# Decoder layer on one Trainium2 core: the opening eight blocks all split, its rows scaled token by token, and raw weights in eight half-size buffers

## The chip, the cores and the metric

The kernel runs on one core of one Trainium2 chip. The metric is device time in microseconds (us) of one execution; the numbers below are medians over executions, and one execution was profiled. TensorE (PE, with its weight loads PEld), VectorE (DVE), ScalarE (ACT), GpSimd (POOL) and SyncE (SP) each work through a queue of their own in program order. All weights come in by DMAs that SP issues.

## The reference

```python
mod = silu(c) @ w_ada + b_ada                      # nine vectors of 1024
sh1, sc1, g1, sh2, sc2, g2, sh3, sc3, g3 = split(mod, 9)
u = rmsnorm(x, norm_ff1) * (1 + sc1) + sh1         # x: 256 tokens x 1024
h = x + 0.5 * g1 * ((silu(u @ w_gate) * (u @ w_up)) @ w_down)     # 2816 hidden columns
u = rmsnorm(h, norm_mix) * (1 + sc2) + sh2
h = h + g2 * token_mixing(u)                       # linear attention and block attention
u = rmsnorm(h, norm_ff2) * (1 + sc3) + sh3
h = h + 0.5 * g3 * swiglu(u)                       # a second feed-forward of the same size
return rmsnorm(h, norm_final)
```

All is float32. The kernel reaches that precision by splitting each operand into a rounded high part and the low part that is left, and summing three products: high x high, high x low, low x high.

## The kernel before

Columns of the model lie on partitions in eight blocks of 128 (k = 0 to 7), tokens along the free axis. A weight tile goes through three steps: a DMA brings it into a raw buffer (`raw`), ACT rounds it (`hi`), DVE subtracts (`lo`). There are four raw buffers of 1 MB and six pairs of `hi` and `lo` of half that width. `split` does the rounding and the subtraction, `mm3` the three matmuls; `Stream` does it for all later weights, two halves to a raw buffer.

This study is about the opening, which here is called the lead. Its input is x, and the first 16 column tiles (8 gate, 8 up) of the first feed-forward. The vectors sc1 and sh1 are needed block by block, so for each k the lead loads 1 MB of `w_ada` (in two loads, `a` pieces), forms two dot products on DVE with `silu(c)` spread over all partitions (`cact`; `ada_dot`), and adds the bias and multiplies the norm weight in (`lead_mods`). It loads 1 MB of gate and up weights in two pieces (`l`), of which 14 column tiles are split and two are used as plain float32 (`lead_native`: TensorE shows two instructions for each). Eight PSUM banks collect all 16 tiles over k.

At the start x is transposed on TensorE into `h`, the square sums of both token tiles give 1/rms (`rstd`: DVE, then POOL), which two more transposes spread over partitions. Then for each block: `lead_normed` (DVE) multiplies by 1/rms, `lead_u` (ACT) applies scale and shift, `lead_uh` (ACT) rounds, `lead_ul` (DVE) subtracts, `lead_mm` runs the matmuls. The string `LEADING` sets the program order of these steps, `LOADS` that of the loads. The lead ends when the matmuls of block 7 are done; the next feed-forward tiles, then down projections, mixing and the second feed-forward follow without a break on TensorE. `mix_constants` and the `w_ada` loads of later vectors (`AdaQueue`) run beside them.

Of the kernel before, what the change touches and what calls it, by code (L numbers as in the profile page):

```python
# [23 lines left out]
NATIVE = 2  # L24
WARM = 5
LOADS = """a00 a01 l00 l01 a10 a11 l10 l11 a20 a21 l20 l21 a30 a31 l30 l31 a40 a41 l40 l41 a50 a51 l50 l51 a60
         a61 l60 l61 a70 a71 l70 l71"""
LEADING = """h00 m0 n0 c0 r00 v0 u0 b t n1 h01 r01 h10 d10 d11 m1 u1 c1 r10 v1 n2 h11 r11 x00 x01 p0 h20 d20 d21 m2
         u2 c2 r20 v2 n3 h21 r21 p1 x10 x11 h30 d30 d31 m3 u3 c3 r30 v3 n4 h31 r31 p2 x20 x21 h40
         d40 d41 m4 u4 c4 r40 v4 n5 h41 r41 p3 x30 x31 h50 d50 d51 m5 u5 c5 r50 v5 n6 h51 r51 p4 x40  # L30
         x41 h60 d60 d61 m6 u6 c6 r60 v6 n7 h61 r61 p5 x50 x51 h70 d70 d71 m7 u7 c7 r70 v7 h71 r71
         p6 x60 x61 A A p7 x70 x71"""
# [8 lines left out]
RAW = 4  # L41
# [36 lines left out]
def hybrid_layer(ctx: ExitStack, tc: tile.TileContext, x, cols, ident_d, tri_d, mask_d, onehot_d,  # L78
                 relT, wlr, ada, lead, gu1, dn1, win, gv, mv, gbr, wout, gu2, dn2, out):
# [80 lines left out]
    def raw_tile():  # L160
        return wp.tile([P, 4 * GV], F32, tag="raw", name=name("raw"), bufs=RAW)

    def load(src, width=2048, parts=1):
        t = raw_tile()
        for i in range(parts):
            sl = slice(i * width // parts, (i + 1) * width // parts)
            nc.sync.dma_start(t[:, sl], src[:, sl] if parts > 1 else src)
        return t

    def split(raw, lo, width=1024, later=False, gap=False):  # L170
# [3 lines left out]
        src, to_hi, to_lo = raw[:, lo:lo + width], hi[:, :width], low[:, :width]  # L174
# [41 lines left out]
    class Stream:  # L216


        def __init__(self):
            self.todo, self.ready, self.raw = [], [], {}  # L220

        def add(self, key, src, which, width=D, parts=1):
            self.todo.append((key, src, which, width, parts))
# [5 lines left out]
        def prepare(self):  # L229
            key, src, which, width, parts = self.todo.pop(0)  # L230
            if key not in self.raw:
                self.raw[key] = load(src, 2 * width, parts)
            self.ready.append(split(self.raw[key], which * width, width, gap=key[0] not in ("gv", "mv")))
# [41 lines left out]
    for t in range(2):  # L275
        nc.sync.dma_start(xt[:, t * D:(t + 1) * D], x[blk(t)])  # L276
    ident = cst.tile([P, P], F32, name="ident")
# [17 lines left out]
    for s in (1, 4, 7):  # L295
        vec.tensor_scalar(bada[:, s, :], bada[:, s, :], 1.0, None, op0=ALU.add)

    cact = cst.tile([P, D], F32, name="cact")
    pc = [bank(), bank()]
    for i in range(KD):  # L300
        ten.transpose(pc[i // 4][:, blk(i % 4)], csil[:, i:i + 1].to_broadcast([P, P]), ident)


    sq, ssq = [mid([P, D]), mid([P, D])], row((P, 8), tag="tiny", bufs=4)
# [35 lines left out]
    class AdaQueue:  # L340
# [5 lines left out]
        def step(self, n=1):  # L346
            for _ in range(n):
# [3 lines left out]
                raw = load(ada[4 * s + q])  # L351
                ada_dot(raw, 0, s, 2 * q)
                ada_dot(raw, D, s, 2 * q + 1)
# [221 lines left out]
    def ada_load(k, i):  # L575
        if i == 0:
            ada_raw[k] = raw_tile()
        sl = slice(0, D) if i else slice(D, 2 * D)
        nc.sync.dma_start(ada_raw[k][:, sl], ada[k, :, sl])  # L579

    def lead_load(k, i):
        if i == 0:
            lead_raw[k] = raw_tile()
        mid_c = (NATIVE + half) * P
        sl = slice(mid_c, N2 * P) if i else slice(0, mid_c)
        nc.sync.dma_start(lead_raw[k][:, sl], lead[k, :, sl])
# [14 lines left out]
    def lead_mods(k):  # L601
        vec.scalar_tensor_tensor(mods[:, 1, k:k + 1], gemv[:, 1, k:k + 1], bada[:, 1, k:k + 1],
                                 colt[:, C_N1 + k:C_N1 + k + 1], op0=ALU.add, op1=ALU.mult)
        vec.tensor_tensor(out=mods[:, 0, k:k + 1], in0=gemv[:, 0, k:k + 1], in1=bada[:, 0, k:k + 1], op=ALU.add)


    def lead_normed(k):
        if k:
            vec.tensor_tensor(out=xn[:, k, :S], in0=h[:, k, :S], in1=lead_rb[0][:, :S], op=ALU.mult)
        else:  # L610
            vec.scalar_tensor_tensor(xn[:, 0, :S], h[:, 0, :S], mods[:, 1, 0:1], rb[:, :S], op0=ALU.mult, op1=ALU.mult)

    def lead_u(k):
        us[k] = row(tag="u", bufs=3)
        act.activation(us[k], xn[:, k, :S], AF.Identity, scale=mods[:, 1, k:k + 1] if k else 1.0, bias=mods[:, 0, k:k + 1])

    def lead_uh(k):
        if k:
            act.activation(uh[:, k, :S], us[k], AF.Copy)
        else:  # L620
            act.activation(uh[:, 0, :S], xn[:, 0, :S], AF.Identity, bias=mods[:, 0, 0:1])

    def lead_ul(k):
        if k:
            vec.tensor_tensor(out=ul[:, k, :S], in0=us[k], in1=uh[:, k, :S], op=ALU.subtract)
        else:
            vec.scalar_tensor_tensor(ul[:, 0, :S], xn[:, 0, :S], mods[:, 0, 0:1], uh[:, 0, :S], op0=ALU.add,
                                     op1=ALU.subtract)
# [3 lines left out]
    def lead_high(k, i):  # L632
        lead_load_until(f"l{k}{i}")
        ws[k, i], rests[k, i] = split(lead_raw[k], (NATIVE + i * half) * P, half * P, True)
# [4 lines left out]
    def lead_native(k):  # L639
        for i in range(NATIVE):  # L640
            b = lead_banks[i // 2]
            mm(b[:, i % 2 * S:(i % 2 + 1) * S], b, lead_raw[k][:, blk(i)], us[k], stop=(k == KD - 1))

    def lead_mm(k, w):
        def to(at):
            i = NATIVE + w * half + at
            return lead_banks[i // 2][:, i % 2 * S:(i % 2 + 1) * S], lead_banks[i // 2]

        if k or w:
            for at in range(half):  # L650
                mm3(*to(at), ws[k, w], blk(at), (uh[:, k, :S], ul[:, k, :S]), stop=(k == KD - 1))
        else:

            for part, rows in ((0, uh), (1, uh), (0, ul)):
                for at in range(half):
                    mm(*to(at), ws[0, 0][part][:, blk(at)], rows[:, 0, :S])

    def lead_rbs():
        act.activation(rbs, rb[:, :S], AF.Copy)
        lead_rb[0] = rbs  # L660

    lead_load_until(to_load[2 * RAW - 1])
    work1 = []
    for f in range(LEAD, NF):
        stream.unit(("gu1", f), gu1[f - LEAD], parts=2 if f == LEAD else 1)
        work1.append(("f", f))
        n = sum(1 for x, _ in work1 if x == "d")
        if n < NF // 2 - 1 and 2 * n + 1 <= f - 2:
            stream.unit(("dn1", n), dn1[n], parts=1 if n else 2)
# [619 lines left out]
```

## Time and profile before

| | |
|---|---|
| median of 3 runs | 572.75 us (571.64 to 572.92) |
| the profiled execution, own time | 572.64 us |
| its span, first to last instruction | 570.9 us |
| TensorE busy | 557.3 us (98%) |
| VectorE busy | 442.8 us (78%) |
| ScalarE busy | 300.8 us (53%) |
| moved by DMA | 140.95 MB, 247 GB/s over the span |

The span leaves out 1.7 us of the execution's own time. Matmul ends are modelled in the profile, so distances between starts say more than TensorE's busy share.

### The profile page before, as it was taken

Reading aid. Unit: us, or ns where it says so; the run is one execution under the profiler, and the core shown is the slowest. Engines: PE = TensorE matmul, PEld = TensorE weight load, DVE = VectorE, ACT = ScalarE, POOL = GpSimd, SP = SyncE. Lnnn points to the kernel's source line nnn. Section 1 sums busy time; section 2 is a strip of 40 time slices with the busy share of each in tenths; the row PEclk is TensorE's granted clock in tenths of the full one; section 3 lists DMA queues with packets and bytes.
Section 4 is the critical chain, followed back from the end, with each engine's and each line's share of the span. In section 5 each row is a group of like instructions: output and inputs, shape, how many; then the busy total and the mean of one; then the engine's idle time right before and its main releaser. Section 6 shows DMA issues by size and latency. Waiting matters only on the chain.

```text
span 570.9 us, 11312 instructions
## 1 busy us (share of the span) xinstructions
PE 557.3 (98%) x4711; PEld 550.1 (96%) x4711; DVE 442.8 (78%) x701; ACT 300.8 (53%) x480; POOL 10.8 (2%) x14
## 2 busy tenths in 40 slices
PE   4999999999999999999999999999999999999996
PEld 3999999999999999998999999999999999999995
DVE  4999887879887896899998979789874656665534
ACT  5455664352536577843764544576644454345424
POOL 0000000000000010000001000001000000000000
PEclk9999999999999999999999999999999999999999
DMA  8999689898989726544489776842796566775102
GB/s 311 357 409 394 255 314 383 302 359 325 325 313 338 242 75 249 193 140 157 130 307 365 287 265 251 309 152 84 284 342 205 195 212 205 254 266 180 67 1 75
DMA packets 23237, 140.95 MB, mean 247 GB/s; under 512 B 2781, under 2 KB 3346, under 8 KB 8850
## 3 DMA queue, kind: packets, MB, share of 16 engines
q1 hardware_dynamic: 22722, 139.37, 67.6%
q8 instruction: 37, 0.61, 0.4%
q0 software_dynamic: 176, 0.53, 0.3%
q10 hardware_dynamic: 288, 0.33, 0.2%
q14 instruction: 14, 0.11, 0.1%
HBM read 139.16 MB, written 1.05 MB: 246 GB/s over the span
## 4 chain that ended last, share of the span: by engine, by line
PE 61%; issue 32%; DVE 4%; DMA 2%; SPq 0%; POOL 0%; ACT 0%; POOLq 0%; DVEq 0%
PE b L103 61%; DMA raw<-in_lead 2%; DVE b L103 1%; DVE lo L103 1%; DVE s L103 1%; DVE raw L103 0%; POOL tiny L363 0%; ACT hi L103 0%; SPq L579 0%; SPq L276 0%; POOLq L1284 0%; DVEq L1284 0%; ACT ub L103 0%; SPq L273 0%; DVE tiny L103 0%
## 5 line engine op out<-in xcount | busy, mean ns | idle before, releaser
L103 PE MATMUL b<-ub,hi 128*128 128x256 f32 (+1 forms) x1888 | 329.3, 279 | 3.2 <-ACT ub L103 3.2
L103 PEld LDWEIGHTS b<-ub,hi 128*128 128x128 f32 x1888 | 286.6, 189 | 5.1 <-ACT ub L103 3.4
L103 DVE TENSOR_TENSOR lo<-raw,hi 128x1024 fp32r<-128x1024 f32 (+2 forms) x188 | 223.2, 1211 | 66.6 <-ACT hi L103 65.1
L103 PE MATMUL b<-ub,lo 128*128 128x256 f32 (+1 forms) x944 | 261.1, 278 | 0.0
L103 ACT ACTIVATE hi<-raw 128x1024 fp32r<-128x1024 f32 (+2 forms) x188 | 191.5, 1044 | 83.4 <-issue 34.4
L103 PEld LDWEIGHTS b<-ub,lo 128*128 128x128 f32 x944 | 177.6, 189 | 0.0
L103 PE MATMUL b<-s,hi 128*128 128x256 f32 x960 | 165.4, 277 | 0.0
L103 PEld LDWEIGHTS b<-s,hi 128*128 128x128 f32 x960 | 144.8, 188 | 0.0
L103 PE MATMUL b<-s,lo 128*128 128x256 f32 x480 | 132.7, 277 | 0.0
L103 PEld LDWEIGHTS b<-s,lo 128*128 128x128 f32 x480 | 90.1, 188 | 0.0
L103 DVE SCALAR_TENSOR_TENSOR raw<-raw,cact 128x1024 f32<-128x1024 f32 x72 | 85.0, 1219 | 2.5 <-DMA raw<-in_ada 2.2
L103 ACT ACTIVATE s<-m 128x256 fp32r<-128x256 f32 x52 | 21.4, 417 | 76.7 <-DVE m L103 76.7
L103 ACT ACTIVATE sg<-b 128x256 f32<-128x256 f32 x46 | 17.0, 379 | 44.9 <-PE b L103 42.9
L103 DVE TENSOR_TENSOR s<-m,s 128x256 fp32r<-128x256 f32 x52 | 21.8, 424 | 20.6 <-ACT s L103 20.5
L103 DVE TENSOR_TENSOR m<-sg,b 128x256 f32<-128x256 f32 x43 | 17.8, 416 | 12.5 <-ACT sg L103 12.2
L103 ACT ACTIVATE s<-b 128x256 f32<-128x256 f32 (+5 forms) x33 | 13.9, 469 | 22.0 <-PE b L103 19.6
L103 PE MATMUL b<-hi,ub 128*128 128x264 f32 (+1 forms) x96 | 21.8, 321 | 0.0
L103 PEld LDWEIGHTS b<-hi,ub 128*128 128x128 f32 x96 | 15.8, 188 | 1.2
L103 PE MATMUL b<-lo,ub 128*128 128x264 f32 (+1 forms) x48 | 15.4, 321 | 0.0
L103 DVE SCALAR_TENSOR_TENSOR b<-b,mods,b 128x256 f32<-128x256 f32 x25 | 11.0, 477 | 4.7 <-PE b L103 4.6
L363 POOL TENSOR_TENSOR tiny<-tiny,mhalf 128x2 f32<-128x2 f32 (+1 forms) x5 | 7.1, 1418 | 365.5 <-DVE tiny L103 365.5
L103 ACT ACTIVATE sq<-b 128x256 f32<-128x256 f32 x24 | 9.2, 407 | 5.6 <-DVE b L103 5.2
(122 smaller groups left out, 276.4 us busy)
## 6 DMA issues: line engine op xcount, KB each, us to landing
raw<-in_gu SPq DMA_DIRECT2D x35, 1024.0 KB, 5.3
raw<-in_ada SPq DMA_DIRECT2D x28, 1024.0 KB, 6.1
raw<-in_dn SPq DMA_DIRECT2D x21, 1024.0 KB, 4.9
raw<-in_win SPq DMA_DIRECT2D x12, 1024.0 KB, 6.4
raw<-in_ada SPq DMA_DIRECT2D x16, 512.0 KB, 7.4
raw<-in_gbr SPq DMA_DIRECT2D x8, 1024.0 KB, 7.2
raw<-in_lead SPq DMA_DIRECT2D x8, 576.0 KB, 6.3
raw<-in_wout SPq DMA_DIRECT2D x4, 1024.0 KB, 5.9
```

Of the source, the lines that this page charges most:

```text
L103: x = getattr(self.engine, op)(*args, **kw)
L363: nc.gpsimd.tensor_tensor(out=rs[:, :n], in0=ms[:, :n], in1=mhalf[:, :n], op=ALU.pow)
```

## The change

Nothing is native any more: the 16 column tiles of each lead block are all split, as two halves of eight (`lead_mm`), with the 32-element gap in the middle of the `hi` and `lo` tiles that the other weights already had. The loads of the lead's `w_ada` rows carry two more columns (input `adal`, rows of 1026 elements) that hold bias and one; `cact` ends in two ones, and the norm weight is the dot product's per-partition scalar, so that the dot products give the finished scale and shift and `lead_mods` goes. The rows of x are scaled by 1/rms while tokens are on partitions (`lead_scaled`), then transposed (`lead_turned`) and copied (`lead_xn`), so `lead_normed` and the spreading of 1/rms go. x itself, transposed, comes later by a load of its own (`xT`, 1 MB, in the first feed-forward). Raw buffers are eight of half the size, and every load is one half, also in `Stream`, `AdaQueue` and `mix_constants`. Transposes of the identity into a bank that nobody reads (`keep_warm`) stand at three places.

```diff
-NATIVE = 2
-WARM = 5
+WARM = (22, 8, 7)
-LEADING = """h00 m0 n0 c0 r00 v0 u0 b t n1 h01 r01 h10 d10 d11 m1 u1 c1 r10 v1 n2 h11 r11 x00 x01 p0 h20 d20 d21 m2
+LEADING = """u0 c0 h00 v0 r00 e1 h01 e2 e3 d10 r01 d11 h10 u1 c1 r10 v1 d20 h11 r11 x00 x01 d21 h20 u2 c2 r20 v2
...
-RAW = 4
+RAW = 8
...
+    def keep_warm(n):
+        for _ in range(n):
+            ten.transpose(warm[:, :P], ident, ident)
+    keep_warm(WARM[0])
     act.activation(sq[0], xt[:, 0:D], AF.Square, accum_out=ssq[:, 0:1])
-    vec.scalar_tensor_tensor(sq[1], xt[:, D:2 * D], 1.0, xt[:, D:2 * D], op0=ALU.mult, op1=ALU.mult,
-                             accum_out=ssq[:, 1:2])
+    act.activation(sq[1][:, 0:512], xt[:, D:D + 512], AF.Square, accum_out=ssq[:, 1:2])
     for i in range(2):
-        act.activation(cact[:, i * 512:(i + 1) * 512], pc[i], AF.Copy)
+        vec.tensor_copy(cact[:, i * 512:(i + 1) * 512], pc[i])
+    vec.scalar_tensor_tensor(sq[1][:, 512:], xt[:, D + 512:2 * D], 1.0, xt[:, D + 512:2 * D], op0=ALU.mult,
+                             op1=ALU.mult, accum_out=ssq[:, 2:3])
...
     def lead_dot(k, i):
-        ada_dot(ada_raw[k], 0 if i else D, 0 if i else 1, k)
+        src = ada_raw[k, i][:, :D + 2]
+        vec.scalar_tensor_tensor(src, src, 1.0 if i else colt[:, C_N1 + k:C_N1 + k + 1], cact, op0=ALU.mult,
+                                 op1=ALU.mult, accum_out=gemv[:, 1 - i, k:k + 1])
...
+    def lead_scaled(t, rest):
+        at = xt[:, t * D + 2 * P:(t + 1) * D] if rest else xt[:, t * D:t * D + 2 * P]
+        if t and rest:
+            vec.tensor_scalar(at, at, rs[:, t:t + 1], None, op0=ALU.mult)
+        else:
+            act.activation(at, at, AF.Copy, scale=rs[:, t:t + 1])
+    def lead_turned(t, rest):
+        for k in range(2, KD) if rest else range(2):
+            ten.transpose(turned_x[k // 2][:, blk(k % 2 * 2 + t)], xt[:, t * D + k * P:t * D + (k + 1) * P], ident)
...
+    lead_dot(0, 0)
+    lead_dot(0, 1)
+    play("s00 t00 s10 t10 s01 w1 e0 s11 t01 t11 w2", {
+        "s": lead_scaled, "t": lead_turned, "e": lead_xn, "w": lambda i: keep_warm(WARM[i])})
...
+        if at == 6:
+            nc.sync.dma_start(h.rearrange("p k s -> p (k s)"), xT)
```

Three places in the order show what moves. First TensorE from the start to the first lead matmul. Before, with `b_1_72` the tile of x, `tiny_152` the 1/rms and `ub_137` the rounded rows (the rows left out repeat the transposes of x):

```order
L103 MATMUL b_95<-ident,csil 128x128 x4
L103 MATMUL b_96<-ident,csil 128x128 x4
L103 MATMUL b_113<-ident,b_1_72 128x128 x2
...
L103 MATMUL b_154<-ident,tiny_152 128x128 x2
L103 MATMUL b_157<-ident 128x128 x5
L103 MATMUL b_167<-ub_137,hi_174 128x256 x2
```

Now, with `b_106` the bank that nobody reads and `ub_75` the rounded rows:

```order
L101 MATMUL b_97<-ident,csil 128x128 x4
L101 MATMUL b_106<-ident 128x128 x22
L101 MATMUL b_159<-ident,b_1_72 128x128 x4
L101 MATMUL b_106<-ident 128x128 x8
L101 MATMUL b_160<-ident,b_1_72 128x128 x2
L101 MATMUL b_162<-ident,b_1_72 128x128 x2
L101 MATMUL b_163<-ident,b_1_72 128x128 x2
...
L101 MATMUL b_106<-ident 128x128 x7
L101 MATMUL b_202<-ub_75,hi_213 128x256
```

The transposes of x have moved behind the scaling; the rows left out are the same three pairs for the second token tile, and they and seven identity transposes now stand directly ahead of the first lead matmul.

Second, DVE from the square sums to the first `lo`. Before, `raw_138` holds `w_ada` rows of block 0, and `b_12_136` is the scaled x:

```order
L103 SCALAR_TENSOR_TENSOR s_5_106,tiny_107<-b_1_72 128x1024
L103 TENSOR_SCALAR tiny_150<-tiny_107 128x2
L103 SCALAR_TENSOR_TENSOR raw_138,gemv<-raw_138,cact 128x1024 x2
L103 SCALAR_TENSOR_TENSOR mods<-gemv,bada,colt 128x1
L103 TENSOR_TENSOR mods<-gemv,bada 128x1
L103 SCALAR_TENSOR_TENSOR b_12_136<-b_7_112,mods,b_154 128x256
L103 TENSOR_TENSOR lo_175<-raw_141,hi_174 128x896
```

Now:

```order
L101 SCALAR_TENSOR_TENSOR s_7_130,tiny_131<-b_1_72 128x512
L101 TENSOR_TENSOR tiny_131<-tiny_131 128x1
L101 TENSOR_SCALAR tiny_155<-tiny_131 128x2
L101 SCALAR_TENSOR_TENSOR raw_139,gemv<-raw_139,colt,cact 128x1026
L101 SCALAR_TENSOR_TENSOR raw_141,gemv<-raw_141,cact 128x1026
L101 TENSOR_SCALAR b_1_72<-b_1_72,tiny_157 128x768
L101 TENSOR_SCALAR u_210<-b_9_138,gemv 128x256
L101 TENSOR_TENSOR ub_75<-u_210,ub_75 128x256
L101 TENSOR_TENSOR lo_214<-raw_143,hi_213 128x2x256 x2
```

The small operations behind the dot products are gone, and the scaling of the last 768 columns of the second token tile stands behind both dot products.

Third, SP's loads of blocks 1 and 2. Before, a buffer takes both pieces:

```order
L579 DMA raw_144<-in_ada 128x1024 x2
L586 DMA raw_147<-in_lead 128x1152
L586 DMA raw_147<-in_lead 128x896
L579 DMA raw_253<-in_ada 128x1024 x2
L586 DMA raw_256<-in_lead 128x1152
```

Now each piece has a buffer of its own:

```order
L163 DMA raw_147<-in_adal 128x1026
L163 DMA raw_149<-in_adal 128x1026
L163 DMA raw_151<-in_lead 128x1024
L163 DMA raw_153<-in_lead 128x1024
L163 DMA raw_237<-in_adal 128x1026
L163 DMA raw_292<-in_adal 128x1026
```

The order of the pieces is the same; the ninth load waits for one half-size buffer instead of a whole one.

## Rows read from the trace of the kernel before

**Rows 1.** Waits of the whole kernel: engine, line, releaser: us, times, longest.
```profile
PE b L103 <- ACT ub L103: 3.2, 1, 3.2
PE b L103 <- ACT csil L103: 3.1, 1, 3.1
```
**Rows 2.** Windows: busy us and instructions by engine, granted clock, DMA share, GB/s.
```profile
14.00:15.00 1.00, 1.00 (x7) 1.00 (x6) 0.65 (x2) 1.00 (x2) 0.00 (x0) 0.50 1.02 418
17.00:18.00 1.00, 1.00 (x11) 1.00 (x10) 1.00 (x3) 0.93 (x1) 0.00 (x0) 1.00 1.03 408
30.00:40.00 10.00, 10.00 (x83) 9.79 (x83) 9.70 (x17) 5.45 (x9) 0.00 (x0) 1.00 1.03 413
60.00:190.00 130.00, 130.00 (x1138) 129.22 (x1137) 106.87 (x154) 62.73 (x89) 1.51 (x2) 1.00 0.89 320
```
**Rows 3.** Timeline of TensorE in the lead: start, us, what.
```profile
13.24 1.68 PE L103 MATMUL b<-ub,hi 128*128 128x256 f32 x7 [3.19 <-ACT ub L103]
21.28 0.58 PE L103 MATMUL b<-ub,hi 128*128 128x256 f32 x2
26.92 0.58 PE L103 MATMUL b<-ub,hi 128*128 128x256 f32 x2
...
55.59 0.39 PE L103 MATMUL b<-ub,hi 128*128 128x256 f32 x2
...
60.01 0.39 PE L103 MATMUL b<-ub,hi 128*128 128x256 f32 x2
```
**Rows 4.** Timeline of TensorE's weight loads, VectorE and SP at the start.
```profile
3.09 1.57 PEld L103 LDWEIGHTS b<-ident,csil 128*128 128x128 f32 x8 [3.09 <-ACT csil L103]
9.22 1.23 DVE L103 SCALAR_TENSOR_TENSOR raw<-raw,cact 128x1024 f32<-128x1024 f32 x1 [1.05 <-DMA raw<-in_ada]
9.23 0.58 PEld L103 LDWEIGHTS b<-ident 128*128 128x128 f32 x5
11.54 0.08 DVE L103 DVE_READ_ACCUMULATOR raw<-raw,cact 128x1 f32 x1
11.65 0.80 SPq L579 DMA_DIRECT2D raw<-in_ada  x2
18.62 0.80 SPq L586 DMA_DIRECT2D raw<-in_lead  x2
```
**Rows 5.** Timeline of ScalarE: the first rounding of a lead block.
```profile
16.97 0.96 ACT L103 ACTIVATE hi<-raw 128x896 fp32r<-128x896 f32 x1 [1.79 <-DMA raw<-in_lead]
29.06 0.95 ACT L103 ACTIVATE hi<-raw 128x896 fp32r<-128x896 f32 x1 [2.79 <-DMA raw<-in_lead]
34.14 0.96 ACT L103 ACTIVATE hi<-raw 128x896 fp32r<-128x896 f32 x1 [2.26 <-DMA raw<-in_lead]
39.23 0.96 ACT L103 ACTIVATE hi<-raw 128x896 fp32r<-128x896 f32 x1 [1.80 <-DMA raw<-in_lead]
```
**Rows 6.** Groups by shape: count | busy us, mean ns of one | idle before.
```profile
L103 DVE SCALAR_TENSOR_TENSOR raw<-raw,cact 128x1024 f32<-128x1024 f32 x72 | 85.0, 1219 | 2.5 <-DMA raw<-in_ada 2.2
L103 DVE TENSOR_TENSOR lo<-raw,hi 128x1024 fp32r<-128x1024 f32 x168 | 201.0, 1222 | 64.6 <-ACT hi L103 63.6 <-PE b L103 0.8
L103 ACT ACTIVATE hi<-raw 128x1024 fp32r<-128x1024 f32 x168 | 172.3, 1053 | 66.7 <-issue 34.4 <-DMA raw<-in_gu 10.2 <-PE b L103 7.3
L103 ACT ACTIVATE u<-b,mods 128x256 f32<-128x256 f32 x8 | 4.7, 589 | 5.2 <-DVE mods L103 5.2
L103 ACT ACTIVATE ub<-u 128x256 fp32r<-128x256 f32 x7 | 2.9, 418 | 0.2
L103 DVE TENSOR_TENSOR ub<-u,ub 128x256 fp32r<-128x256 f32 x7 | 3.0, 426 | 0.6
L103 DVE TENSOR_SCALAR s<-s,tiny 128x256 f32<-128x256 f32 x4 | 1.4, 346 | 0.0
```
**Rows 7.** DMA issues: what, count, KB each, median us from issue to landing.
```profile
raw<-in_win SPq DMA_DIRECT2D x12, 1024.0 KB, 6.4
raw<-in_gv SPq DMA_DIRECT2D x2, 1056.0 KB, 7.7
```

More of the change, by code (lines that the diff above doesn't have):

```diff
@@ L77, in hybrid_layer @@
 @with_exitstack
-def hybrid_layer(ctx: ExitStack, tc: tile.TileContext, x, cols, ident_d, tri_d, mask_d, onehot_d,
-                 relT, wlr, ada, lead, gu1, dn1, win, gv, mv, gbr, wout, gu2, dn2, out):
+def hybrid_layer(ctx: ExitStack, tc: tile.TileContext, x, xT, cols, ident_d, tri_d, mask_d, onehot_d,
+                 relT, wlr, adal, ada, lead, gu1, dn1, win, gv, mv, gbr, wout, gu2, dn2, out):
     nc = tc.nc
@@ L229, in prepare @@
         def prepare(self):
[L230 to L233, printed above, removed]
+            key, src, which, width = self.todo.pop(0)
+            raw = load(src[:, which * width:(which + 1) * width])
+            self.ready.append(split(raw, width, gap=key[0] not in ("gv", "mv")))
         def ahead(self, n):
@@ L350, in step @@
                 s, q = self.todo.pop(0)
[L351 to L353 removed]
+                for i in range(2):
+                    ada_dot(load(ada[4 * (s - 2) + q, :, i * D:(i + 1) * D]), s, 2 * q + i)
                 if q == KD // 2 - 1:
@@ L575, in ada_load @@
     def ada_load(k, i):
[L576 to L579, printed above, removed]
+        ada_raw[k, i] = load(adal[k, i])
     def lead_load(k, i):
[L582 to L586, printed above, removed]
+        lead_raw[k, i] = load(lead[k, :, i * D:(i + 1) * D])
     to_load = LOADS.split()
@@ L633, in lead_high @@
         lead_load_until(f"l{k}{i}")
-        ws[k, i], rests[k, i] = split(lead_raw[k], (NATIVE + i * half) * P, half * P, True)
+        ws[k, i], rests[k, i] = split(lead_raw[k, i], later=True, gap=True, pieces=1 if k or i else 2)
     def lead_low(k, i):
         rests[k, i]()
[L639 to L642, printed above, removed]
     def lead_mm(k, w):
[L645 to L662, printed above, removed]
+        rows = uh, ul
+        order = [(at, *p) for at in IN_TURN for p in ((0, 0), (0, 1), (1, 0))]
+        if k == 1 and w == 0:
+            order = [(at, *p) for p in ((0, 0), (1, 0), (0, 1)) for at in IN_TURN]
+        if k == 0:
+            halves = (IN_TURN,) if w else (IN_TURN[:4], IN_TURN[4:])
+            order = [(at, 0, r) for part in halves for r in (0, 1) for at in part] + [(at, 1, 0) for at in IN_TURN]
+        for at, part, r in order:
+            b = lead_banks[4 * w + at // 2]
+            mm(b[:, at % 2 * S:(at % 2 + 1) * S], b, ws[k, w][part][:, wblk(at)], rows[r][:, k, :S],
+               stop=(k == KD - 1 and part == 1))
+    lead_load_until(to_load[RAW - 1])
     work1 = []
     for f in range(LEAD, NF):
-        stream.unit(("gu1", f), gu1[f - LEAD], parts=2 if f == LEAD else 1)
+        stream.unit(("gu1", f), gu1[f - LEAD])
         work1.append(("f", f))
@@ L1243, in _packed @@
     rows = w["w_ada"][0].T.reshape(9, KD, P, D)
-    first = rows[:2].transpose(1, 2, 0, 3).reshape(KD, P, 2 * D)
-    d["ada"] = _c(np.concatenate([first, _units(rows[2:].reshape(7 * KD, P, D))], 0))
+    more = np.zeros((2, KD, P, 2), np.float32)
+    more[:, :, :, 0] = w["b_ada"][0].reshape(9, KD, P)[:2]
+    more[1, :, :, 1] = 1.0
+    d["adal"] = _c(np.concatenate([rows[:2], more], 3)[::-1].transpose(1, 0, 2, 3))
+    d["ada"] = _units(rows[2:].reshape(7 * KD, P, D))
     for n in ("1", "2"):
@@ L1263, in _packed @@
     return d
-_INS = ["x", "cols", "ident", "tri", "mask", "onehot", "relT", "wlr", "ada", "lead", "gu1", "dn1", "win",
+_INS = ["x", "xT", "cols", "ident", "tri", "mask", "onehot", "relT", "wlr", "adal", "ada", "lead", "gu1", "dn1", "win",
         "gv", "mv", "gbr", "wout", "gu2", "dn2"]
```

111 lines of the change are left out of this document (49 added, 62 removed).

## The prediction

> **What bounds the kernel now.** I read the waits first. TensorE's only waits of a microsecond or more lie before its matmuls have got going, the longest 3.2 us for the first rounded rows [rows 1]. So whatever the change does elsewhere is hidden unless TensorE starts to wait; a time can only come out of the lead, or be lost by a wait that isn't there today. The windows then give the pace behind the lead: from 60 to 190 us 1138 matmuls in 130 us, one every 0.114 us, with the DMAs moving 320 GB/s, against 413 GB/s from 30 to 40 us in the lead [rows 2]. So the stretch behind the lead asks for about three quarters of what the DMAs have shown they can give.
>
> In the lead itself the timeline shows three things [rows 3]. The first matmul starts at 13.24, block 1 at 21.28, block 2 at 26.92, and the first matmul behind the lead at 60.01. From block 1 to block 2 it is 5.64 us. And 13 groups of three split matmuls take 60.01 - 55.59 = 4.42 us, so a group takes 0.340. The granted clock is 0.50 from 14 to 15 us, that is 1.2 GHz, and 1.00 (2.4 GHz) from 17 to 18 [rows 2]: TensorE had stood idle for 3.19 us ahead of 13.24 [rows 3], and block 0 is largely worked off at the low level, with 7 matmuls in that window against 11 in the later one. VectorE is busy for 9.70 of 10 us [rows 2], so it is nearly a second bound, and ACT waits for the DMA at each block's first piece [rows 5].
>
> **The change, part by part.** The sum is made on when the matmuls behind the lead can start.
>
> *When block 0 starts.* The loads ahead of it keep their order and nearly their size, so the first dot product still starts about 9.22 and the second ends about 11.54, put off by some 0.08 for the two more columns and the scalar taken per partition: 11.62 [rows 4]. The end of 1/rms moves a little earlier (VectorE squares 512 columns instead of 1024), but it is not what ends last, since the scaling of the second tile's 768 columns stands behind both dot products in VectorE's queue. No row has that shape. A scaling of 256 columns takes 0.346 [rows 6]; that is the lower bound, three times that, 1.04, the upper. The fixed part can't be paid three times, so I take 0.6, which gives 12.2. Behind it TensorE has six transposes of x and seven of the identity. Five identity transposes were loaded in 0.58 us, 0.116 each; the eight of `csil`, the first work TensorE does, took 1.57, 0.20 each [rows 4]. These two are my bounds. With TensorE busy shortly before I take 0.116: 13 x 0.116 = 1.5, and 0.1 for the hand-over. Block 0 starts at 13.8, half a microsecond later than now. Its rounded rows and weights are there by then: the rows come from ACT 0.42 after 11.62, and the first half of `hi` within 0.6 more [rows 6]. The scaled x and its copies end earlier still.
>
> *The clock.* Before that start TensorE now has 22 transposes right behind those of `csil`, then scattered ones up to 13.8, so its longest idle time is the one between the 22 and the first scaled rows. Those of `csil` end at about 4.7; the 22 take 2.6 us at 0.116 or 4.4 at 0.20, so they end between 7.3 and 9.1. 1/rms is no later than now, when its transposes are over by 9.23 [rows 4]; with 0.35 for the first scaling the next transposes come by 9.6. So TensorE idles for 0.5 to 2.3 us, against the 3.19 us behind which the clock was low. I take block 0 at 2.4 GHz throughout. That is what the waits for identity transposes buy, and the largest term.
>
> *The pace.* Sixteen groups of 0.340 make a block 5.44 us, against 5.64 with fourteen groups and two native tiles: 0.2 less. Eight blocks from 13.8: 43.5 us, the lead ends at 57.3 instead of 60.01. **Gain 2.7 us.** TensorE's order inside block 0 and 1 costs nothing by itself, the matmul count being the same.
>
> *Can VectorE follow?* Per block it has two dot products and two `lo` of 1024, at 1.22 each with about 0.07 overlapped from one to the next, and the subtraction of 0.43 [rows 6]: 2 x 1.15 + 2 x 1.15 + 0.4 = 5.0, below 5.44. Gone are `lead_mods` and `lead_normed`; the wider `lo` takes some of it back. ACT has 2 x 1.05 + 0.59 + 0.42 = 3.1 [rows 6].
>
> *Can the DMAs follow?* Block 1's first weights are there at 16.97, those of blocks 3, 4 and 5 at 29.06, 34.14 and 39.23 [rows 5], 5.09 us apart: the DMA's own pace for 2 MB. Between block 1 and 3 it lost 29.06 - 16.97 - 2 x 5.09 = 1.9 us. The reason is in SP's rows: the reload of block 0's weight buffer was issued only at 18.62, when both its halves had been subtracted, 7 us behind the load before it [rows 4]. With half-size buffers each reload waits for its own half; VectorE ends those of block 0 at about 14.3 (12.2, then 0.35 for the row, 0.43, and 1.3 for two half `lo`) and 16.7 (then a dot product and a `lo`), so the queue doesn't run dry. I let block 2 land at 22.1 and block 7 at 47.5. From landing to the first matmul it is 1.05 + 0.59 + 0.42, plus 0.43 for the second [rows 6], 2.5 us: block 2 could start at 24.6 (wanted at 24.7), block 7 at 50.0 (wanted at 51.9). So it just holds at block 2, and better later.
>
> *The smaller loads behind the lead.* The DMA's packet per row becomes 4 KB instead of 8. The lead's loads have such rows already and reached 413 GB/s [rows 2]; behind it 320 are wanted. I take nothing. The Trainium skill speaks against this part: "DMA: Bandwidth & Descriptors", section Bandwidth, wants at least 1 MB in a DMA, as each pays about 2 us beside its bytes. By that page's figures an estimate for 512 KB alone is 3.2 us, and for 40 MB behind the lead, one load at a time, 250 us, over 100 more than TensorE leaves; overlapped in the queue they cost nothing. The lead's loads of about 512 KB came four in 5.09 us [rows 5], so here they do overlap.
>
> *xT* adds 1 MB to those 130 us, 8 GB/s; it waits for nothing that is late. The three loads for `tri` put the small `onehot` load later, but TensorE wants it four work items behind the lead (4 x 5.44 = 22 us), so I take 0, at most 1.
>
> The rest of TensorE's program is the same instruction for instruction, so it follows 2.7 us earlier. On the profiled execution's own 572.64 us that makes **570.0 us**; the median of the runs is 0.1 above it.
>
> **The rivals.**
>
> *Rows of 1026 elements are slow to load.* Their 4104 bytes start at no round address, and no such load is in the trace. Let each cost e us more. The last block's weights then land at 47.5 + 16e, and the lead ends at least 2.5 + 5.44 later: 55.4 + 16e. Up to e = 0.12 nothing is lost; at 0.29 the whole gain is; above that the kernel is slower than before. Lower bound 0. Upper bound from the nearest rows: the two loads of `gv`, with rows of odd length, needed 7.7 us to landing, those of `win` 6.4 [rows 7], 20% more; on an average of 5.09 / 4 = 1.27 us a load that is e = 0.26, the lead ends at 59.6 and the time is 572.2. As much again, e = 0.5, gives 63.4 and 576.0. `gv` may only have met a fuller queue, so I stay near zero. The Trainium skill has a rule for it, "DMA: Bandwidth & Descriptors", section How a descriptor splits into AXI transactions: a row that doesn't begin at a multiple of 256 bytes fetches bytes that nobody uses. No run here shows that yet. By it an estimate is one or two transactions more on 16, e about 0.08 to 0.16, the lead's end at 57.3 to 58.0, the time 570.0 to 570.6. I give 0.25 to a cost of this kind between 570.8 and 572.4, and 0.06 to one above.
>
> *The clock falls all the same.* If TensorE is at 1.2 GHz when block 0 starts, it stays there for about as long as now, from 13.24 to some time in 16 to 17: 3.3 us in which half the work is done, 1.7 us lost, and up to 13 x (0.20 - 0.116) = 1.1 at the transposes. The lead ends at 59 to 60, the time is 571.7 to 572.7. For it: the 1/rms comes from POOL, whose spans are rough. Against it: the idle time is at most 2.3 us, where 3.19 stood ahead of 13.24. Chance 0.1.
>
> *Half-size loads starve the first feed-forward.* The DMAs are busy for 0.89 of those 130 us [rows 2], so 14 us are free; xT takes 2.6 of them. Some 40 loads of 1 MB become 80. Each of the 40 more could cost 0.28 us before TensorE waits, and 0.35 before the kernel is slower than now; at 0.5 us it is 578. Nothing in the lead speaks for it. Chance 0.04, with whatever else the queue order may do.
>
> *More than the forecast*: if the scaling takes 0.4 and the transposes 0.1, and the finer buffers spare waits in the mixing stage, 568.8 to 569.4. Chance 0.08.
>
> **How the numbers follow.** The forecast, 569.4 to 570.8, has 0.47. What a measurement of this kernel can tell from no change is about 0.2%, 1.1 us, so faster means under 571.6: the forecast, the better case, and two thirds of the slow rows' 0.25, 0.71 in all. The rest of these, and most of the clock's, come to 0.2 for the same. Slower, above 573.9, takes 0.09: slow rows beyond e = 0.37, starved loads, and 0.02 for what I don't see. The range that leaves out no more than 2 in 10 is 569.2 to 572.5.
>
> **What would show it.** Right: granted clock 1.00 from 13 us on; the first lead matmul at 13.5 to 14.1, behind a scaling that waited for the second dot product; 5.44 us from block to block; the matmuls behind the lead at 57 to 57.6, and no TensorE wait behind it that is not there today. Wrong: ACT waiting for `in_adal` or `in_lead` loads up to block 7 and TensorE for ACT; loads of `adal` that take longer than those of `lead` beside them; a clock row of 0.50; DVE waiting for `ada` loads in the first feed-forward.

## The result and the profile after

The changed kernel takes 568.38 us (median, 568.30 to 568.83) against 572.83 us for the kernel before beside it: ratio 0.9929, 95% interval [0.9912, 0.9946], 4.45 us less. Forecast were 570.0 us, 2.7 us less, with a range from 569.2: the kernel is faster, and by more than the range held. The profiled execution took 568.44 us with a span of 566.7, 4.2 less than the 570.9 of before.

The longest wait on TensorE, 3.2 us for the first rounded rows [rows 1], is gone. In the view of the waits TensorE's longest is now

```profile
PE b L101 <- ACT csil L101: 3.1, 1, 3.1
```

The windows that answer to [rows 2], in the same columns:

```profile
13.00:14.00 1.00, 1.00 (x11) 1.00 (x10) 1.00 (x3) 1.00 (x3) 0.00 (x0) 1.00 1.02 410
14.00:15.00 1.00, 1.00 (x11) 1.00 (x10) 1.00 (x1) 1.00 (x3) 0.00 (x0) 1.00 1.09 295
30.00:40.00 10.00, 10.00 (x91) 10.00 (x90) 9.88 (x14) 5.85 (x9) 0.00 (x0) 1.00 1.03 408
60.00:190.00 130.00, 130.00 (x1143) 129.22 (x1142) 106.06 (x150) 63.19 (x88) 1.51 (x2) 1.00 0.92 333
```

The granted clock is 1.00 where it was 0.50. But look at the last row too: 1143 matmuls in the 130 us behind the lead, where there were 1138. That stretch was forecast to move, not to get shorter.

TensorE's timeline in the lead, as [rows 3] (here every block is 16 groups of three matmuls):

```profile
13.37 2.10 PE L101 MATMUL b<-ub,hi 128*128 128x256 f32 x16
...
24.49 0.38 PE L101 MATMUL b<-ub,hi 128*128 128x256 f32 x1
25.15 0.39 PE L101 MATMUL b<-ub,hi 128*128 128x256 f32 x1 [0.27 <-DVE ub L101]
...
30.63 0.39 PE L101 MATMUL b<-ub,hi 128*128 128x256 f32 x2
...
57.83 0.39 PE L101 MATMUL b<-ub,hi 128*128 128x256 f32 x2
```

Block 0 starts at 13.37, block 2 at 24.49 with a stall of 0.66 us behind its first matmul, block 3 at 30.63, and the lead ends at 57.83. (57.83 - 30.63) / 5 = 5.44 us a block, as forecast. The timelines of ScalarE, VectorE and SyncE's queue, as [rows 4, 5]:

```profile
16.31 1.06 ACT L101 ACTIVATE hi<-raw 128x1024 fp32r<-128x1024 f32 x1 [0.75 <-DMA raw<-in_lead]
22.44 1.06 ACT L101 ACTIVATE hi<-raw 128x1024 fp32r<-128x1024 f32 x1 [2.94 <-DMA raw<-in_lead]
27.61 1.06 ACT L101 ACTIVATE hi<-raw 128x1024 fp32r<-128x1024 f32 x1 [2.22 <-DMA raw<-in_lead]
32.74 1.06 ACT L101 ACTIVATE hi<-raw 128x1024 fp32r<-128x1024 f32 x1 [2.04 <-DMA raw<-in_lead]
...
9.77 1.23 DVE L101 SCALAR_TENSOR_TENSOR raw<-raw,cact 128x1026 f32<-128x1026 f32 x1
10.92 0.62 DVE L101 TENSOR_SCALAR b<-b,tiny 128x768 f32<-128x768 f32 x1
23.53 1.23 DVE L101 TENSOR_TENSOR lo<-raw,hi 128x1024 fp32r<-128x1024 f32 x1 [1.03 <-ACT hi L101]
24.67 0.42 DVE L101 TENSOR_TENSOR ub<-u,ub 128x256 fp32r<-128x256 f32 x1
...
14.00 1.53 SPq L163 DMA_DIRECT2D raw<-in_lead  x2
```

Block 2's weights come at 22.44; rounding, scale and shift, and two subtractions later its rows are there at 25.1, and TensorE has waited. Reloads start at 14.00 instead of 18.62, as planned.

**Where the time came from.** The lead ends 60.01 - 57.83 = 2.18 us earlier. The span is 4.2 shorter. So 2.0 us come from behind the lead, where TensorE runs the same instructions in the same order. Put side by side, the two traces' matmuls drift apart evenly: 2.2 us at 65, 2.4 at 100, 2.8 at 198, 3.4 at 366, 4.0 at 540. TensorE's timeline where a feed-forward item (one tile's run of matmuls) begins, before (rows from `s`, the hidden tiles, then from `ub`):

```profile
425.14 0.28 PE L103 MATMUL b<-s,lo 128*128 128x256 f32 x1
425.26 0.40 PE L103 MATMUL b<-ub,hi 128*128 128x256 f32 x2
...
425.61 0.40 PE L103 MATMUL b<-ub,hi 128*128 128x256 f32 x2
...
425.97 0.40 PE L103 MATMUL b<-ub,hi 128*128 128x256 f32 x2
...
426.32 0.39 PE L103 MATMUL b<-ub,hi 128*128 128x256 f32 x2
426.55 0.28 PE L103 MATMUL b<-ub,lo 128*128 128x256 f32 x1
426.66 0.39 PE L103 MATMUL b<-ub,hi 128*128 128x256 f32 x2
```

and the same item after:

```profile
421.67 0.28 PE L101 MATMUL b<-s,lo 128*128 128x256 f32 x1
421.78 0.39 PE L101 MATMUL b<-ub,hi 128*128 128x256 f32 x2
...
422.12 0.39 PE L101 MATMUL b<-ub,hi 128*128 128x256 f32 x2
...
422.46 0.39 PE L101 MATMUL b<-ub,hi 128*128 128x256 f32 x2
```

After, a group of three takes 0.34 us from the first; before, the first three take 0.35 to 0.36, 117 to 118 ns a matmul instead of 113.3, and only then 0.34. No row shows a wait. In the kernel before, this stands at nearly every change from `s` rows to `ub` rows and back, 6 to 9 matmuls long.

The same instructions, then, but not the same places. The abridged diff ahead of the prediction left out a line that moved:

```diff
     for t in range(2):
         nc.sync.dma_start(xt[:, t * D:(t + 1) * D], x[blk(t)])
+    uh, ul = parts_tile()
...
     xn = big()
-    uh, ul = parts_tile()
```

Tiles lie in each partition in the order of their first use in the code. Before, `ub` lay behind the ten `s4` tiles (shown as `s`) and four `tiny` tiles of 32 bytes, 128 bytes past a multiple of 256 from `s4`. Now `ub` lies in front of `s4`, a multiple of 256 away. And `cact`, wider by 64 columns, has moved what lies behind it by 256 bytes, `hi` and `lo` among it.

### The profile page after: what moved, and what is told of

Same layout as the page of the kernel before. It is cut to its first block, busy times and chain, and to the rows that moved or that the text cites. A ratio compares the mean times of both kernels' runs of the same rounds, so it can differ in the third digit from the quotient of the medians.

```text
span 566.7 us, 11731 instructions
## 1 busy us (share of the span) xinstructions
PE 556.5 (98%) x4757; PEld 550.1 (97%) x4757; DVE 442.1 (78%) x683; ACT 304.5 (54%) x484; POOL 10.8 (2%) x14
## 4 chain that ended last, share of the span: by engine, by line
PE 59%; issue 32%; DVE 5%; DMA 2%; ACT 1%; POOL 0%; SPq 0%; POOLq 0%; DVEq 0%
PE b L101 59%; DVE lo L101 2%; DMA raw<-in_lead 1%; DVE b L101 1%; DVE s L101 1%; DMA b<-in_x 1%; DVE raw L101 0%; POOL tiny L361 0%; ACT b L101 0%; ACT hi L101 0%; POOLq L1277 0%; DVEq L1277 0%; ACT ub L101 0%; DVE tiny L101 0%; SPq L276 0%
## 5 line engine op out<-in xcount | busy, mean ns | idle before, releaser
L101 ACT ACTIVATE hi<-raw 128x1024 fp32r<-128x1024 f32 (+2 forms) x189 | 193.8, 1049 | 69.9 <-issue 32.0
L101 DVE SCALAR_TENSOR_TENSOR raw<-raw,cact 128x1024 f32<-128x1024 f32 (+1 forms) x64 | 75.9, 1221 | 0.0
L101 ACT ACTIVATE s<-b 128x256 f32<-128x256 f32 (+5 forms) x34 | 14.5, 474 | 25.1 <-PE b L101 22.0
```

Source lines behind the costliest of these rows:

```text
L101: x = getattr(self.engine, op)(*args, **kw)
```

## The experiments

Times are medians beside the kernel before on the same chip, with the ratio to it. Where a run is set against the changed kernel, that is the 568.38 us above, taken apart from these runs; `e8_after_cold`, `e12_all32` and `e13_after_pad256`, taken on three chips, came out within 0.12 us of it. A table at the end of the second part gathers the places.

**Which part of the change quickens the pace behind the lead?** Four kernels change one thing each.

`e1_shift`, the kernel before:

```diff
-    cact = cst.tile([P, D], F32, name="cact")
+    cact = cst.tile([P, D + 64], F32, name="cact")[:, :D]
```

> The kernel before with cact 64 columns wider (unused), so that raw, hi, lo, b8, s4 and ub all begin 256 bytes higher in each partition; nothing else. Theory PLACE-256 (the pace behind the lead hangs on where hi and lo lie): 2 us faster, 570.8 us, and of the matmul distances behind the lead hardly any at 116 to 123 ns. Theories PLACE-UB (it hangs on where ub and s4 lie) and LOADS (it hangs on the size of the loads): no change, 572.8 us, some 12% of distances at 116 to 123 ns as in the kernel before.

Measured: 572.57 us, 0.9999 [0.9987, 1.001]. Moving everything together by 256 bytes does nothing.

`e2_ub`, the kernel before with the line moved:

```diff
+    uh, ul = parts_tile()
     ident = cst.tile([P, P], F32, name="ident")
...
     xn = big()
-    uh, ul = parts_tile()
```

> The kernel before with the tile of the rounded rows (ub) placed ahead of the s4 tiles instead of behind them, by one call written earlier; hi and lo stay. PLACE-UB: 2 us faster, 570.8 us, distances even. PLACE-256 and LOADS: 572.8 us, no change.

Measured: 570.85 us, 0.9978 [0.9964, 0.9993], with even distances behind the lead. Its trace gives 1.7 us there; the profiled execution's lead ended at 60.5, later than before.

`e3_half_loads`, the kernel before:

```diff
-    def load(src, width=2048, parts=1):
+    def load(src, width=2048, parts=2):
...
-        def add(self, key, src, which, width=D, parts=1):
+        def add(self, key, src, which, width=D, parts=2):
```

(and the two calls that named `parts`; the load of `tri` stays whole)

> The kernel before with every 1 MB load behind the lead made as two of 512 KB into the two halves of the same raw buffer, rows of 4 KB instead of 8; all tiles stay where they are. LOADS: 2 us faster, 570.8 us, distances even, since smaller packets disturb TensorE's reads less. Both PLACE theories: 572.8 us, uneven as before.

Measured: 572.31 us, 0.9999 [0.999, 1.0009], distances uneven as before. Twice as many loads of half the size neither help nor harm.

`e4_ub_back`, the changed kernel with the line moved back:

```diff
-    uh, ul = parts_tile()
     ident = cst.tile([P, P], F32, name="ident")
...
     xn = big()
+    uh, ul = parts_tile()
```

> The changed kernel with ub placed behind s4 again, as in the kernel before; hi and lo stay 256 bytes up, loads stay 512 KB. PLACE-UB: 2 us slower than the changed kernel, 570.4 us, 116 to 123 ns back. PLACE-256 and LOADS: 568.4 us, even distances.

Measured: 570.62 us, 0.9966 [0.9953, 0.9978]; the uneven distances are back. So one moved line makes the second gain. This kernel is also the lead's part of the change alone: 572.26 - 570.62 = 1.6 us by the medians, while its traced lead ends at 57.46, 2.5 earlier than that of before.

**Is it the order of the tiles or their distance?** An unused tile between `ub` and `s4` tells:

```diff
     uh, ul = parts_tile()
+    wk.tile([P, 32], F32, tag="pad", name="pad", bufs=1)
```

That is `e6_after_pad128`; 16, 64 and 8 columns make `e7_after_pad64`, `e13_after_pad256` and `e14_after_pad32`. `e5_pad128` has the 128 bytes in the kernel before, in front of `ub`, which lies behind `s4` there:

```diff
+    wk.tile([P, 32], F32, tag="pad", name="pad", bufs=1)
     uh, ul = parts_tile()
```

`e15_both_64` has the same edit with 16 columns in the changed kernel, where `ub` and `s4` then move together.

> The kernel before with an unused tile of 128 bytes in front of ub, so that ub starts a multiple of 256 bytes behind the s4 tiles; hi, lo, s4 and the loads stay. Theory SOURCE (a switch of the moving operand between ub and s4 costs some 5 ns on each of the next 6 to 9 matmuls when their places differ by 128 bytes modulo 256, and nothing when they don't): 1.5 to 2 us faster than the kernel before, and no run of 116 to 123 ns distances where a feed-forward item begins. Rival ORDER (what counts is that ub lies below s4, or which region it lies in): no change, 116 to 123 ns stay.

Measured: 570.49 us, 0.9962 [0.995, 0.9974]. An empty tile of 128 bytes makes the kernel before 2.4 us faster by the medians, over the 1.5 to 2 expected, and 1.8 by the traces, with `ub` still behind `s4`.

> The changed kernel with an unused tile of 128 bytes between ub and s4. SOURCE: 1.5 to 2 us slower than the changed kernel, 570.0 to 570.4 us, with runs of 116 to 123 ns at each switch between ub and s4. ORDER: 568.4 us as the changed kernel, even distances.

Measured: 570.33 us, 0.9965 [0.9952, 0.9977], 1.95 slower than the changed kernel. ORDER has fallen.

> The changed kernel with an unused tile of 64 bytes between ub and s4. SOURCE says nothing firm on a difference of 64 bytes modulo 256: as slow as with 128 (570.0 to 570.4 us) if any difference counts, 568.4 us if only that of 128 does. ORDER: 568.4 us.

Measured: 577.10 us, 1.0076 [1.0063, 1.0089]. 64 bytes cost 8.7 us, more than the whole change brings, and neither of the times expected. In its trace not only the switches are slow: nearly all matmuls with rows from `s4` are, throughout their items. There `s4` begins at the same place modulo 128 bytes as `hi` and `lo`, which led to the next three.

> The changed kernel with an unused tile of 256 bytes between ub and s4. SOURCE (the difference of their places counts modulo 256 bytes): 568.4 us as the changed kernel, distances of 113.3 ns. Rival EXACT (the changed kernel's distance of 20480 bytes is a lucky one, any pad spoils it): 570 us or more.

Measured: 568.44 us, 0.9918 [0.9903, 0.9933], as the changed kernel. The distance counts modulo 256.

> The changed kernel with an unused tile of 32 bytes between ub and s4. 128 cost 2.0 us and 64 cost 8.7. WEIGHTS (the large loss comes where the rows lie at the same place modulo 128 bytes as the weights; 32 bytes doesn't put them there) with SOURCE (any other difference costs a switch): about 570.4 us. If the loss falls off with the distance alone: between 568.4 and 570.4 us.

Measured: 576.87 us, 1.0067 [1.0052, 1.0082]. That is a miss: 32 bytes cost 8.5 us, nearly what 64 cost. So the same place as the weights isn't the only bad one. Whether it is the 96 bytes to the weights or the 32 to `ub` that does the harm, this run can't tell, since both are new in it.

> The changed kernel with an unused tile of 64 bytes ahead of ub, so that ub and s4 both move up by 64 and keep their distance, and both come to lie at the same place modulo 128 bytes as hi and lo. WEIGHTS: nearly every split matmul takes 117 to 120 ns instead of 113.3; 5.5 ns on some 1440 matmuls with rows from s4 and 2450 from ub behind the lead are 21 us, and up to 2 us in the lead: 588 to 592 us. Rival SWITCH (only the change of source costs): 568.4 us.

Measured: 590.37 us, 1.0315 [1.029, 1.0339], 22 us slower than the changed kernel, as WEIGHTS had it. Here are windows over the same 100 us, in the columns of [rows 2]. The kernel before:

```profile
400.00:500.00 100.00, 100.00 (x881) 100.00 (x880) 66.28 (x83) 48.83 (x65) 0.00 (x0) 1.00 0.70 242
```

The changed kernel:

```profile
400.00:500.00 100.00, 100.00 (x885) 100.00 (x884) 66.17 (x84) 47.75 (x65) 0.00 (x0) 1.00 0.75 249
```

The changed kernel with both moved by 64 bytes:

```profile
400.00:500.00 100.00, 100.00 (x843) 100.00 (x842) 66.59 (x89) 50.06 (x73) 0.00 (x0) 1.00 0.66 218
```

TensorE is busy for all 100 us in each, at granted clock 1.00, with no wait; only the count of matmuls (881, 885, 843) tells. The split matmuls behind the lead, from the traces (mean distance in ns from one start to the next, and how many were 116 ns or longer), with the places in bytes:

```
                 ub to s4   rows to weights   rows from s4        rows from ub         us
                 mod 256    mod 128 (s4, ub)
before             128        64, 64          113.9, 168 of 1438  114.3, 428 of 2434   572.8
e5_pad128            0        64, 64          113.3,   0 of 1438  113.9, 222 of 2435   570.5
after                0        64, 64          113.3,   0 of 1431  113.9, 208 of 2422   568.4
e6_after_pad128    128        64, 64          114.1, 222 of 1433  114.2, 355 of 2422   570.3
e7_after_pad64      64         0, 64          118.9, 1233 of 1429 114.2, 363 of 2422   577.1
e14_after_pad32     32        96, 64          118.4, 1255 of 1437 114.3, 383 of 2422   576.9
e15_both_64          0         0,  0          118.9, 1284 of 1438 119.0, 2161 of 2429  590.4
```

The sum works out: before to after, 1438 x 0.60 + 2434 x 0.46 ns = 2.0 us; for `e7_after_pad64`, 1429 x 5.5 + 2422 x 0.35 ns = 8.7 us.

`e12_all32`, the changed kernel, moves every tile from `raw` to `s4` by 32 bytes:

```diff
-    cact = cst.tile([P, D + 64], F32, name="cact")[:, :D + 2]
+    cact = cst.tile([P, D + 72], F32, name="cact")[:, :D + 2]
```

> The changed kernel with every tile from raw to s4 moved up by 32 bytes, so that all places are the same to each other, but hi, lo, ub and s4 start at multiples of 64 bytes instead of 32 above one. SOURCE (only the places of the operands to each other count): 568.4 us, distances of 113.3 ns. Rival ABSOLUTE (the place in the partition counts): another pace of the matmuls behind the lead, up or down, 564 to 577 us.

Measured: 568.38 us, 0.9925 [0.9906, 0.9944], distances of 113.3 ns. So the places to each other count; the place in the partition changed nothing, here or in `e1_shift`.

**What made the lead shorter?** Four kernels on the terms of the sum.

`e8_after_cold`, the changed kernel:

```diff
-WARM = (22, 8, 7)
+WARM = (0, 0, 0)
```

> The changed kernel without its 37 transposes of the identity (they feed nothing). Theory CLOCK (without them TensorE stands idle for some 5 us between csil and the first scaled rows and block 0 runs at 1.2 GHz): granted clock 0.50 in the first lead block, 1.7 to 2.8 us slower than the changed kernel, 570.1 to 571.2 us. Rival NO CLOCK (the transposes in between and block 0 itself bring the level up in time, and seven transposes less ahead of block 0 let it start up to 0.8 us earlier): 567.6 to 568.6 us.

Measured: 568.26 us, 0.9922 [0.9909, 0.9935]. CLOCK's forecast of the time has fallen: the 37 transposes bring nothing. Windows:

```profile
12.00:13.00 1.00, 1.00 (x7) 1.00 (x6) 1.00 (x2) 1.00 (x3) 0.00 (x0) 1.00 1.02 415
13.00:14.00 1.00, 1.00 (x7) 1.00 (x6) 0.95 (x2) 1.00 (x2) 0.00 (x0) 1.00 0.99 390
14.00:15.00 1.00, 1.00 (x10) 1.00 (x10) 1.00 (x3) 0.86 (x2) 0.00 (x0) 1.00 1.07 332
```

Block 0 begins at 12.73, at half pace (7 matmuls a us, 214 ns apart) until 13.94, then at full pace. The clock column is no evidence here: this trace holds its first record of the clock at 14.09 us, and the column shows 1.00 where there is none. In the trace of before matmuls were 213 to 214 ns apart where a record says 0.50 [rows 2], so TensorE was very likely at the low level. That made block 0 6.27 us long instead of 5.56, and the start 0.64 us earlier pays for it: block 2 begins at 24.45, as in the changed kernel. Its rows come in time there, and it takes 5.54 us instead of 6.14. The lead ends at 57.36.

`e9_before_warm`, the kernel before:

```diff
-WARM = 5
+WARM = 32
```

> The kernel before with 32 instead of 5 transposes of the identity ahead of block 0, which fill its 3.2 us of idle time (they feed nothing). CLOCK (the low level in block 0 is what the lead lost): granted clock 1.00 from 13 us on, the lead ends 1.7 us earlier, at 58.3, and the time is 1.7 us less than that of the kernel before. SUPPLY (blocks 2 and 3 wait for weights that land at 22.7 and 28.9 whatever TensorE does): clock 1.00 too, but block 3 starts no earlier than about 31.4, the lead ends at 58.9, 1.1 us less. If the clock cost nothing: 0.

Measured: 573.43 us, 1.0016 [0.9998, 1.0033]: no gain. From its timeline:

```profile
13.89 1.07 PE L103 MATMUL b<-ub,hi 128*128 128x256 f32 x7
...
16.80 0.40 PE L103 MATMUL b<-ub,hi 128*128 128x256 f32 x2
...
17.15 0.40 PE L103 MATMUL b<-ub,hi 128*128 128x256 f32 x2
...
60.48 0.40 PE L103 MATMUL b<-ub,hi 128*128 128x256 f32 x2
```

The granted clock was 1.00 from 13 us on. Against the trace of before TensorE started 0.65 later and at 16.86 was 0.88 ahead, so the low level there had cost 1.5 us. But its groups of three took 0.355 us through the lead (16.80 to 17.15) where those of before take 0.340, and the lead ended at 60.48. This run doesn't settle what the clock was worth in the kernel before: another slowness took its place, with 118 ns a matmul as above, for a reason that I did not find. It isn't the places, which are those of the kernel before. `e3_half_loads` has them too, and in its trace all 21 matmuls with rows from `ub` between 17 and 21 us were 116 ns or longer, against 3 of 23 in that of before.

`e10_pairs`, the changed kernel:

```diff
+    raw_pair = []
+
     def raw_tile():
-        return wp.tile([P, 2 * GV], F32, tag="raw", name=name("raw"), bufs=RAW)
+        if not raw_pair:
+            t = wp.tile([P, 4 * GV], F32, tag="raw", name=name("raw"), bufs=RAW // 2)
+            raw_pair.extend([t[:, 2 * GV:], t[:, :2 * GV]])
+        return raw_pair.pop()
```

> The changed kernel with its raw buffers tied in pairs again: two loads of 512 KB share one of four 1 MB buffers, so that a reload waits for both halves. SUPPLY: the DMAs run dry between 19 and 22 us as in the kernel before, the weights of block 3 land 1.3 to 1.9 us later, the lead ends at 59.1 to 59.7 and the time is 569.7 to 570.3 us. Rival (TensorE's start decides, the buffers' size is hidden): 568.4 us. Behind the lead nothing in either.

Measured: 569.75 us (568.15 to 571.05), 0.9949 [0.993, 0.9968], 1.4 slower than the changed kernel by the medians. One of its seven runs was as fast as the changed kernel, the others were 0.96 us slower or more. SUPPLY has its size, and is wrong on the place: the DMAs fall off from 24 us on, not at 19.

```profile
24.00:25.00 1.00, 1.00 (x12) 1.00 (x11) 1.00 (x2) 0.97 (x3) 0.00 (x0) 1.00 0.98 336
25.00:26.00 1.00, 1.00 (x11) 1.00 (x10) 1.00 (x2) 0.61 (x1) 0.00 (x0) 1.00 0.98 328
27.00:28.00 1.00, 1.00 (x11) 1.00 (x10) 1.00 (x2) 0.46 (x1) 0.00 (x0) 1.00 0.85 328
```

The changed kernel moved 412 GB/s from 26 to 28 us. The loss reaches TensorE late: blocks 3, 4 and 5 start as in the changed kernel (30.65, 36.09, 41.53), blocks 5 and 6 lose 0.1 us each, and at block 7 the weights have fallen far enough behind to stall it. Its first rounding, released by the load, and TensorE at its start:

```profile
50.58 1.06 ACT L101 ACTIVATE hi<-raw 128x1024 fp32r<-128x1024 f32 x1 [3.25 <-DMA raw<-in_lead]
...
52.64 0.38 PE L101 MATMUL b<-ub,hi 128*128 128x256 f32 x1
53.29 0.38 PE L101 MATMUL b<-ub,hi 128*128 128x256 f32 x1 [0.27 <-DVE ub L101]
```

In the changed kernel that rounding starts at 48.09:

```profile
48.09 1.06 ACT L101 ACTIVATE hi<-raw 128x1024 fp32r<-128x1024 f32 x1 [2.04 <-DMA raw<-in_lead]
```

The lead of the profiled execution ended at 58.72, 0.9 later than that of the changed kernel.

`e11_order`, the changed kernel, in blocks 2 to 7 (block 2 shown):

```diff
-d21 h20 u2 c2 r20 v2
+d21 u2 c2 h20 v2 r20
```

> The changed kernel with scale, shift and rounding of the rows (u, c) put ahead of the rounding of the weights (h) on ScalarE in blocks 2 to 7, and the rows' subtraction (v) ahead of the weights' (r) on VectorE. SUPPLY (block 2 starts when the last link behind its weights' landing is through, and this shortens the chain by the 1.0 us of u and c, to h and r): the stall at block 2 shrinks by about 0.6 us or goes, the lead ends at 56.8 to 57.3, the time is 567.4 to 567.9 us. Rival (TensorE alone sets the lead's end): 568.4 us.

Measured: 576.67 us, 1.0065 [1.0043, 1.0087]: 8.3 slower than the changed kernel. Both theories missed. The timeline of ScalarE and VectorE around block 3:

```profile
29.96 0.60 ACT L101 ACTIVATE u<-b,gemv 128x256 f32<-128x256 f32 x1 [3.84 <-DVE raw L101]
30.60 0.42 ACT L101 ACTIVATE ub<-u 128x256 fp32r<-128x256 f32 x1
30.92 1.99 ACT L101 ACTIVATE hi<-raw 128x1024 fp32r<-128x1024 f32 x2
...
28.70 1.22 DVE L101 SCALAR_TENSOR_TENSOR raw<-raw,cact 128x1026 f32<-128x1026 f32 x1
31.05 0.42 DVE L101 TENSOR_TENSOR ub<-u,ub 128x256 fp32r<-128x256 f32 x1 [1.12 <-ACT ub L101]
32.00 1.23 DVE L101 TENSOR_TENSOR lo<-raw,hi 128x1024 fp32r<-128x1024 f32 x1 [0.52 <-PE b L101]
```

Rounding the weights used to fill ScalarE's wait for the second dot product. With it behind the rows, ScalarE waits 3.84 us for VectorE, then VectorE 1.12 for ScalarE, in every block: 6.79 us a block instead of 5.44. A chain that is shorter for one block can be longer as a loop.

## Why the prediction was wrong

The step of the prediction that failed is the last of the sum: "The rest of TensorE's program is the same instruction for instruction, so it follows 2.7 us earlier." The instructions are the same; their operands lie elsewhere, and the stretch behind the lead became 2.0 us shorter by itself. `e2_ub`, `e4_ub_back`, `e5_pad128` and `e6_after_pad128` show that 1.4, 2.2, 2.4 and 2.0 us hang on the places of `ub` and `s4` alone. Without it the change gives 570.3 to 570.6, inside the forecast's 569.4 to 570.8. No rival was of this kind. The row to look at was there: TensorE busy throughout and 1138 matmuls in 130 us are 114.2 ns apiece, where the lead's groups give 113.3. (Not all of that gap was to be had: the changed kernel's 1143 are 113.7.)

Point by point:

- *When block 0 starts*: forecast 13.8, measured 13.37. The scaling of 768 columns took 0.62 (taken: 0.6). It began at 10.92 rather than 11.62: in this trace the rows of `w_ada` were there earlier than before, and the dot products waited for no load. That varies: in the traces of `e12_all32` and `e13_after_pad256`, which take the same time as the changed kernel, block 0 starts at 12.47 and 14.11, and the lead ends at 57.58 and 57.86. So within this range the start hardly moves the lead's end.
- *The clock*: right as a reading (1.00 from 13 us on), mis-sized as a term. It was called the largest; `e8_after_cold` loses nothing without what buys it: its block 0 is 0.71 us longer, but starts 0.64 earlier, with seven transposes less ahead of it (and starts vary, as the first point says). That run had half pace for only 1.2 us of block 0, however, so it doesn't price the 3.3 us of the kernel before.
- *The pace*: 5.44 us from block 3 on, as forecast; blocks 0 and 1 took 5.56.
- *Can VectorE and the DMAs follow?* "So it just holds at block 2" did not come true in this trace: block 2 wanted to start at 24.49, its rows came at 25.1. Block 2's weights landed at 22.44, not 22.1, and rounding, which stands ahead of scale and shift, kept the rows back. With 0.43 us from the earlier start, 0.24 lost in blocks 0 and 1 and 0.7 in block 2 the lead ended at 57.83 instead of 57.3: a gain of 2.18, not 2.7.
- *Half-size buffers*: right in kind; `e10_pairs` prices them at 1.4 us by medians, 0.9 by the lead's end in the trace.
- *The smaller loads behind the lead*: nothing, as taken (`e3_half_loads`). The Trainium skill's rule of at least 1 MB a load ("DMA: Bandwidth & Descriptors", section Bandwidth) did not show in the time of these overlapping loads: 0.9999 [0.999, 1.0009].
- *Rows of 1026 elements*: not slow. First roundings of blocks 2 to 4 stand 5.17 and 5.13 us apart, against 5.09 before; e is 0.02 to 0.04 us a load.

What stays open is the mechanism by which places set the pace. Shown is that two differences count behind the lead: `ub` to `s4` modulo 256, by 128 bytes against 0, and rows to weights modulo 128, by 0 against 64. The 96 bytes of `e14_after_pad32` are mixed with a new distance to `ub`. Of the 208 slow ones that the changed kernel keeps, some 120 have rows of 258 elements instead of 256; these took about 120 ns in the kernel before as well (124 of 134 were slow there). Nearly all the 208 lie between 190 and 310 us and between 370 and 400, and hardly any in the feed-forward items before and behind. Why a switch costs 6 to 9 slower matmuls, why rows of 258 are slow, and why `e9_before_warm` ran its lead at 118 ns, no run tells. Offsets other than these were not tried.

## What to carry to other kernels

"The same instructions" is not "the same time": a widened tile or an allocation moved up shifts what lies behind it, so compare the distance from matmul to matmul, and the places of rows and weights modulo 128 and 256 bytes, before giving a gain to the logic of an edit. TensorE's busy share hides this, since a slow matmul counts as busy; count matmuls per window in a stretch that should not have changed. And price a term only after asking what waits next: an earlier start is worth little where the weights come late. Where a clock column reads 1.00, ask whether the trace holds a record for that time; the distance between matmuls tells.

## What the runs showed of the hardware

With float32r rows of 256 and 128x128 weights in a steady stream behind the lead at granted clock 1.00, a matmul took 113.3 ns with the rows 64 bytes (modulo 128) from the weights (`e13_after_pad256`, rows from `s4`) and 118.9 at 0 (`e15_both_64`). At 96, with the other source 32 bytes away, it took 118.4 (`e14_after_pad32`). The places aren't all of it: the lead of `e9_before_warm` ran at 118 ns with 64 bytes. A switch between two sources of rows 128 bytes apart (modulo 256) cost about 5 ns on each of the next 6 to 9 matmuls, and nothing at 0 (`e5_pad128`, `e13_after_pad256`). And TensorE ran at half pace, 214 ns a matmul, until 13.94 us in `e8_after_cold`, behind 3.9 us of idle time and 16 transposes; in the kernel before, with a record of 0.50, matmuls were 213 to 214 ns apart.
